# Plain float32 products in place of three products of split operands, in one layer of attention, convolution and mixture of experts

## The chip, the cores and the metric

The kernel runs on one NeuronCore of a Trainium2 chip. The metric is the device time of one execution, in microseconds (us). The names of the engines are those of the profile: PE is the tensor engine's matrix products (PEld its weight loads, which run beside them), DVE the vector engine, ACT the scalar engine, POOL the GpSimd engine, SP the sync engine, which here only issues DMAs.

## The reference

One layer over 1024 tokens of width 1024, all in float32. Cut to what matters here:

```python
h = rmsnorm(x, norm1_g) * (1 + sc1) + sh1              # sh1, sc1, gt1, ...: from c by one product (adaLN)
z = h @ w_in                                           # 1024 x 3744
q_lat, kv_lat, k_rope, conv_in, gate_logits = split(z) # 384, 256, 32, 1024, 2048 columns
q  = rmsnorm(q_lat, q_norm_g) @ w_uq                   # 8 heads of 64 + 32 (the 32 are rotated)
kv = rmsnorm(kv_lat, kv_norm_g) @ w_ukv                # 8 heads of 64 (keys) + 64 (values)
y_attn = causal_attention(q, k, v) @ w_o_attn          # 512 -> 1024
u = glu_a * sigmoid(glu_b)                             # glu_a, glu_b: the halves of conv_in
u = silu(layernorm(causal_depthwise_conv(u, 31 taps)))
y_conv = u @ w_conv_out                                # 512 -> 1024
g_attn, g_conv = split(sigmoid(gate_logits))
x = x + gt1 * ((g_attn * y_attn + g_conv * y_conv) @ w_out)
h = rmsnorm(x, norm2_g) * (1 + sc2) + sh2
# 32 experts in 4 groups: each token takes its best group, and in it its best 2 experts
x = x + gt2 * sum_over_2(weight * (silu(h @ e_gate) * (h @ e_up)) @ e_down)  # 1024 -> 128 -> 1024
out = rmsnorm(x, final_norm_g)
```

## The kernel before

**How float32 products are made.** The tensor engine has two ways to take 32-bit operands: as plain float32, and as the type float32r, a float32 whose low bits don't count. The kernel before makes most of its large products out of float32r operands. Each operand A is kept as two tiles, a high part Ah (ACT casts A to float32r) and a low part Al = A - Ah (a subtraction on POOL or DVE), and the product A B is added up in PSUM from three passes, Ah Bh, Ah Bl and Al Bh. That is `mm3` (L104 to L107); below it is called a triple. The names of the tiles end in h and l: hT0h, hT0l, wg0h, wg0l and so on. A triple makes 128 x 512 outputs out of 128 terms each, except where another width is said. The transposes, the products of the attention's probabilities with the values (mo), the experts' gate and up products (pe) and the router's are plain float32 already.

**The stages, in the order of the program, with their span in the profiled execution and their triples:**

- *0 to 65 us.* x is loaded, normalised and transposed. DVE and PE compute the adaLN vectors as their weights arrive. hT is the normalised, modulated and transposed x in two halves of tokens (n = 0, 1). The first products of the convolution's input start: 32 triples, written as `prod_h` and `prod_l` (L593, L600: lines L597, L598, L603 in the trace).
- *65 to 154 us.* The rest of the convolution's input: for each of 4 blocks of channels j and each half n two products of 8 triples (pa and pb), 96 triples. A GLU (`glu`, L543) makes u[j] from pa and pb, and DVE then goes through the 31 taps of the depthwise convolution (`conv_taps`, L748; one instruction of 128 x 1024 per tap and block, L757), which go on until 292 us. The weights are loaded and split by `wtile` (L507) and `w_split` (L503). The latents' weights wl are split here too (L783 on ACT, L784 on POOL).
- *154 to 214 us.* The latents z (L792): for each of 8 tiles of tokens one product of 384 columns and one of 288, 8 triples each.
- *214 to 416 us.* The 2 x 1024 branch gates (L868 on): 16 blocks of columns by 2 halves by 8 triples, 256 triples. The tanh of each goes to DRAM (gscr). When 6 blocks are issued, the convolution's output cacc is transposed (cT, L834), normalised, and turned into the split tiles csh and csl.
- *416 to 471 us.* `conv_out` (L923): 64 triples, whose result times the gate goes to DRAM (mscr). The latents come back, are normalised and transposed into split tiles; the weights of queries, keys and values are prepared and split.
- *471 to 659 us.* Attention: 16 triples for keys, 48 for queries, 16 for values; the scores (`softmax`, L1046) take 48 triples of 512 columns and 16 each of 384, 256 and 128. Each query, key and attention output is split in turn.
- *659 to 716 us.* The merge (from L1315): the attention's projection w_o_attn, 64 triples (pm), times the gates from DRAM, plus the convolution's branch. The sum yT is split. `split_wout` (L1308) scales each block of w_out by gt1 and splits it.
- *716 to 830 us.* The output projection (`out_mm`, L1486; po): 128 triples. The residual, second norm and router of a tile run beside the products of later tiles.
- *830 to 842 us.* The routing of the last tile and the tables of tokens by expert; `keep_warm` (L1397) issues plain float32 products of no use (warmmm, warmtr) while PE would wait.
- *842 to 1053 us.* The experts (`expert`, L1635), 28 of them one by one with up to 128 rows: gather the rows by an indirect DMA (xg, POOL), transpose them (xp), modulate (xT), gate and up products (pe), the hidden values hid on ACT and DVE, their split (hdh, hdl), the split of the down weights (rdh, rdl: L1654, L1655), two groups of triples of 512 columns for the down product (pd), the scaled result ob on DVE, and an indirect DMA that adds its rows to yscr in DRAM (L1705). The last 4 experts share two blocks of rows; their results are kept on chip as split tiles kh and kl.
- *1053 to 1094 us.* For each tile of tokens the kept rows are added by products with a 0-1 matrix km (pk, L1842: kh and kl, two passes each), then the final norm.

**What sets the order.** Within `manual_schedule` (the loads on SP throughout, the start, the attention's and the output projection's PE work) the program's order is the engine's order. Elsewhere a scheduler orders the instructions of each engine when the program is built, by a simulated timeline. Tiles with one tag share a number of buffers; named slots S0 to S17, R0 to R19 and W0 to W8 of 4 KB per partition are handed on from use to use, and a slot's new tile waits for the last reader of the old one. `seq` (L1431) lists the slots into which the experts' weights are loaded, in order; its first entries are loaded ahead, before the routing is known.

Of the kernel before, what the change touches and what calls it, by code (L numbers as in the profile page):

```python
# [15 lines left out]
F32R = mybir.dt.float32r  # L16
# [35 lines left out]
def hybrid_layer(ctx: ExitStack, tc: tile.TileContext, x, c, positions, ada_w, ada_b, norm1_g,  # L52
# [106 lines left out]
    # constants  # L159
# [24 lines left out]
    # vectors that are wanted as columns: one stack of rows, one transpose  # L184
# [27 lines left out]
    # rotary tables, [token, tile, frequency]  # L212
# [73 lines left out]
    # positions: mask of the diagonal blocks, and whether the tiles follow one another  # L286
# [42 lines left out]
    hpool, hpool_s = open_pool("hpool", "left")  # L329
    hT = [[hpool.tile([P, KD, 512], F32R, name=f"hT{n}{s}") for s in "hl"] for n in range(2)]  # L330
# [28 lines left out]
    def x_square(t):  # L359
        A.activation(hT[1][1][:, 2 * (t % 4):2 * (t % 4) + 2].rearrange("p a b -> p (a b)"), xts[t], AF.Square,  # L360
                     accum_out=ms[:, t:t + 1])
# [16 lines left out]
    def x_trans(n, k):  # L378
        p = ps_tr(f"xT{n}{k}")
        for i in range(4):  # L380
            PE.transpose(p[:, i * P:(i + 1) * P], xts[4 * n + i][:, k * P:(k + 1) * P], ident)
        xn[n, k] = sb.tile([P, 512], F32, name=f"xn{n}{k}", tag="xn", bufs=8)
        return p
# [15 lines left out]
    def ada_load(j):  # L399
# [3 lines left out]
                  3: [(sa, "raw", 3), (sb, "b4", 3)] + [(sa, "raw", 3)] * 2, 4: [(cvp, "cu", 4)] * 4}[j]  # L403
# [96 lines left out]
    def lo_part(lo, full, hi, eng=G):  # L500
        eng.tensor_tensor(lo, full, f32(hi), op=OP.subtract)

    def w_split(w, hi, lo):  # L503
        A.copy(hi, w)
        lo_part(lo, w, hi)

    def wtile(name, src, split=True, parts=1, raw=None):  # L507
        w = (raw or sa).tile([P, KD, P], F32, name=name, tag="b4" if raw else "raw", bufs=3)
# [40 lines left out]
    def conv_w2(j, split=True, parts=1, raw=None):  # L549
        return (w_cols(f"wa{j}", C0 + j * P, split, parts, raw), w_cols(f"wb{j}", C0 + CC + j * P, split, parts, raw))  # L550
# [11 lines left out]
    # loads, in the order in which they are wanted  # L562
# [1375 lines left out]
```

## Time and profile before

| what | value |
|---|---|
| time, median of 3 runs | 1100.92 us |
| lowest, highest | 1093.43, 1104.52 us |
| span of the profiled execution | 1093.9 us |
| PE, DVE, ACT, POOL busy in it | 995.7, 796.1, 437.3, 422.0 us |
| mean granted TensorE clock in it | 0.95 of full speed |

The span is the time from the profiled execution's first instruction to its last; no other time is given for that execution. It is 0.5 us above the lowest of the three runs and 7.0 us below their median. Busy times of different engines overlap. A matmul record lasts longer than the time until the next one starts, since matmuls are pipelined: what a product costs is read from start to start.

### The profile page before, as it was taken

The page shows a single profiled execution, that of the slowest core. Times are in us where ns is not written, and L with a number is a line of the kernel's source. Part 1 is how long each engine was busy: PE and PEld are TensorE (multiplying, and loading weights), DVE is VectorE, ACT ScalarE, POOL GpSimd, SP SyncE. Part 2 cuts the span into 40 slices and gives each one's busy share as a digit, 9 for nine tenths or more (in the row PEclk, how much of TensorE's full clock was granted, in tenths as well). Part 3 has the DMA queues.
Part 4 walks back from the last instruction along what each step waited for, and adds up shares of the span by engine and source line. Part 5 has one row for each costly group of instructions (what it writes and reads, how often), then busy time and mean ns, then how long its engine had stood idle before and what let it go on. Part 6 is the DMA issues. An engine that isn't in the chain of part 4 may idle for free. (4 is left out here: it accounts for less than half of the span.)

```text
span 1093.9 us, 16693 instructions
## 1 busy us (share of the span) xinstructions
PE 995.7 (91%) x5744; PEld 841.5 (77%) x5744; DVE 796.1 (73%) x1839; ACT 437.3 (40%) x914; POOL 422.0 (39%) x361
## 2 busy tenths in 40 slices
PE   4697979999599999999999998899998999999991
PEld 2576869988477788778888877678886999997881
DVE  7989999999989815547556665964447888875555
ACT  4453312212123334347666773232223555543343
POOL 5555929823121114114333446630004464454111
PEclk9798989999899999999999999999999999997876
DMA  9902521246574263710000016684656989998813
GB/s 305 307 8 58 140 70 37 92 159 183 172 228 140 105 213 130 249 41 1 1 2 17 6 59 200 212 300 163 258 189 240 314 284 282 301 272 227 269 77 155
DMA packets 97743, 176.79 MB, mean 162 GB/s; under 512 B 14123, under 2 KB 53116, under 8 KB 97648
## 3 DMA queue, kind: packets, MB, share of 16 engines
q1 hardware_dynamic: 82736, 148.33, 40.8%
q0 software_dynamic: 9152, 16.28, 6.3%
q10 hardware_dynamic: 5760, 11.01, 2.8%
q8 instruction: 48, 0.79, 0.3%
q14 instruction: 47, 0.39, 0.1%
HBM read 145.22 MB, written 40.35 MB: 170 GB/s over the span
## 5 line engine op out<-in xcount | busy, mean ns | idle before, releaser
L757 DVE SCALAR_TENSOR_TENSOR cacc<-u,cw,cacc 128x1024 f32<-128x1024 f32 x120 | 173.2, 1496 | 0.0
L1676 PE MATMUL pe<-xT,rg 128*128 128x128 f32 (+7 forms) x512 | 78.9, 288 | 0.1
L1676 PEld LDWEIGHTS pe<-xT,rg 128*128 128x128 f32 x512 | 73.2, 204 | 5.6 <-ACT xT L1671 0.5
L1671 ACT ACTIVATE xT<-xp,h2c 128x128 f32<-128x128 f32 (+7 forms) x128 | 52.4, 434 | 53.4 <-DVE xT L1668 28.8
L1676 PE MATMUL pe<-xT,ru 128*128 128x128 f32 (+7 forms) x512 | 68.8, 293 | 0.0
L1676 PEld LDWEIGHTS pe<-xT,ru 128*128 128x128 f32 x512 | 66.0, 209 | 0.0
L1705 POOL DMA_INDIRECT yscr<-ob,srci x18 | 33.6, 1868 | 59.4 <-DVE ob L1699 30.4
L105 PE MATMUL po<-woh,y 128*128 128x512 f32 x128 | 53.7, 419 | 1.4 <-DVE gm L1331 1.4
L1668 DVE TENSOR_SCALAR xT<-xp,h2c 128x128 f32<-128x128 f32 (+7 forms) x128 | 45.4, 381 | 10.3 <-ACT xT L1671 9.9
L107 PE MATMUL po<-woh,y 128*128 128x512 f32 x128 | 50.4, 394 | 0.0
L106 PE MATMUL po<-wol,y 128*128 128x512 f32 x128 | 50.3, 393 | 0.0
L873 ACT ACTIVATE gt<-pg 128x512 f32<-128x512 f32 x32 | 19.0, 594 | 68.9 <-PE pg L107 68.9
L1518 POOL TENSOR_SCALAR x1n<-x,rst 128x1024 f32<-128x1024 f32 x8 | 9.0, 1121 | 93.9 <-DVE rst L127 82.4
L479 DVE SCALAR_TENSOR_TENSOR acc<-aw,cact,acc 128x1024 f32<-128x1024 f32 x28 | 39.8, 1421 | 3.2 <-DMA aw<-in_ada_w_dram 3.2
L1663 PE MATMUL xp<-ident,xg 128*128 128x128 f32 (+7 forms) x256 | 39.0, 276 | 1.8 <-DMA xg<-xscr,si 1.8
L1655 DVE TENSOR_TENSOR rdl<-rd,rdh 128x1024 fp32r<-128x1024 f32 x30 | 36.7, 1223 | 5.3 <-ACT rdh L1654 5.2
L1654 ACT CAST rdh<-rd 128x1024 fp32r<-128x1024 f32 x30 | 31.4, 1045 | 18.9 <-PE pd L107 17.8
L1081 PE MATMUL mo<-pT,V 128*64 128x128 f32 x576 | 38.5, 278 | 0.0
L1699 DVE SCALAR_TENSOR_TENSOR ob<-pd,wvp,gt2b 128x512 f32<-128x512 f32 (+7 forms) x36 | 26.4, 744 | 16.6 <-DMA yscr<-ob,srci 12.5
L1663 PEld LDWEIGHTS xp<-ident,xg 128*128 128x128 f32 (+7 forms) x256 | 33.5, 194 | 4.0 <-DVE eid L1619 2.6
L1332 POOL TENSOR_TENSOR gm<-gm 128x512 f32<-128x512 f32 x16 | 27.5, 1726 | 22.0 <-DVE gm L1331 19.4
L1081 PEld LDWEIGHTS mo<-pT,V 128*64 128x64 f32 x576 | 30.8, 136 | 5.7 <-issue 5.7
(2071 smaller groups left out, 3141.2 us busy)
## 6 DMA issues: line engine op xcount, KB each, us to landing
aw<-in_ada_w_dram SPq DMA_DIRECT2D x32, 512.0 KB, 3.8
rg<-in_expert_w_gate_dram SPq DMA_DIRECT2D x32, 512.0 KB, 9.6
ru<-in_expert_w_up_dram SPq DMA_DIRECT2D x32, 512.0 KB, 9.2
rd<-in_expert_w_down_dram SPq DMA_DIRECT2D x32, 512.0 KB, 9.3
x<-in_x_dram SPq DMA_DIRECT2D x16, 512.0 KB, 5.5
ad<-in_ada_w_dram SPq DMA_DIRECT2D x32, 256.0 KB, 5.5
wg<-in_w_in_dram SPq DMA_DIRECT2D x16, 512.0 KB, 4.9
gscr<-gt ACTq DMA_DIRECT2D x32, 256.0 KB, 2.9
```

What stands on the lines that cost most here:

```text
L105: PE.matmul(ps, lh, rh, start=first, stop=False)
L106: PE.matmul(ps, lh, rl, start=False, stop=False)
L107: PE.matmul(ps, ll, rh, start=False, stop=last)
L479: V.scalar_tensor_tensor(acc, w, cact[:, k:k + 1], acc, op0=OP.mult, op1=OP.add)
L757: V.scalar_tensor_tensor(a, u[j][:, k:k + T], cw[:, j, k:k + 1], a, op0=OP.mult, op1=OP.add)
L1081: PE.matmul(po[par * DV:(par + 1) * DV, i % 4 * P:(i % 4 + 1) * P], Vt[b][:, 2 * pr + par], pTs[par][:, b * P:(b + 1) * P], start=(b == 0) ...
L1655: V.tensor_tensor(rdl, rd, f32(rdh), op=OP.subtract)
L1663: PE.transpose(p[:, c], xv[:, k, :], ident[:m, :m])
L1668: split_.append(V.tensor_scalar(xT[:, ks], p[:, c], h2c[:, 0, k:k + 1], h2c[:, 1, k:k + 1], op0=OP.mult, op1=OP.add).ins)
L1671: A.activation(xT[:, ks], p[:, c], AF.Identity, scale=h2c[:, 0, k:k + 1], bias=h2c[:, 1, k:k + 1])
L1676: PE.matmul(pa[:, o:o + m], w[:, k * P:(k + 1) * P], xT[:, k * P:k * P + m], start=(k == 0), stop=(k == KD - 1))
L1705: s_ = G.indirect_dma_start(out=yscr, out_offset=bass.IndirectOffsetOnAxis(ap=src[:m], axis=0), in_=ob[:m], in_offset=None, bounds_check=T ...
```

## The change

Every triple becomes one `PE.matmul` of plain float32 operands. With it go the split tiles, the casts on ACT that made the high parts and the subtractions on POOL and DVE that made the low parts; single float32 tiles take their places. With the room this leaves:

- `raw`, the buffers of the input projection's weights, are 9 instead of 3 (the split tiles wh and wl had 4 each); the latents' weights have places of their own; `conv_out` has 5 buffers for weights and gates instead of 3; the merge has 4 places for its gates instead of 3.
- The slots W0 to W8 are opened before the attention instead of after it, and w_o_attn is loaded into W0 to W3, one load each, where it stayed split in W0 to W7 by way of W8.
- yT takes 8 slots instead of 16, and w_out 8 instead of 16; half of yT's sums move from POOL to DVE. The factor 0.5 that went into yT's split goes into gt1.
- `seq` gives 37 slots before one is used again, instead of 32.
- The kept experts' products pk are one float32 product in place of two float32r passes (kh, kl).

The order of the stages stays. The diff, cut to one place of each kind:

```diff
-    def mm3(ps, lh, ll, rh, rl, first, last):
-        PE.matmul(ps, lh, rh, start=first, stop=False)
-        PE.matmul(ps, lh, rl, start=False, stop=False)
-        PE.matmul(ps, ll, rh, start=False, stop=last)
...
     def second_half(k, p):
-        A.activation(xn[1, k], p, AF.Identity, scale=s1[:, k:k + 1], bias=ada[:, k:k + 1])
-        A.copy(hT[1][0][:, k], xn[1, k])
-        lo_part(hT[1][1][:, k], xn[1, k], hT[1][0][:, k])
+        A.activation(hT[1][:, k], p, AF.Identity, scale=s1[:, k:k + 1], bias=ada[:, k:k + 1])
...
-    def w_split(w, hi, lo):
-        A.copy(hi, w)
-        lo_part(lo, w, hi)
...
     def proj_k(p, w, n, k):
-        mm3(p, w[0][:, k], w[1][:, k], hT[n][0][:, k], hT[n][1][:, k], k == 0, k == KD - 1)
+        PE.matmul(p, w[:, k], hT[n][:, k], start=k == 0, stop=k == KD - 1)
...
     for k in range(KD):
-        w = sa.tile([P, NL], F32, name=f"wl{k}", tag="raw", bufs=3)
+        w = sl.tile([P, NL], F32, name=f"wl{k}")
         SY.dma_start(w, w_in2[k * P:(k + 1) * P, :NL])
-        hi = sl.tile([P, NL], F32R, name=f"wlh{k}")
-        lo = sl.tile([P, NL], F32R, name=f"wll{k}")
-        A.copy(hi, w)
-        G.tensor_tensor(lo, w, f32(hi), op=OP.subtract)
-        wl.append((hi, lo))
+        wl.append(w)
...
     def proj_query(tg, h, n, latT, q, v):
         p = bank(f"{tg}uq{h}{n}", "up", 2)
         for k in range(3):
-            mm3(p, wq[k][0][:, h], wq[k][1][:, h], latT[n][0][:, k], latT[n][1][:, k], k == 0, k == 2)
-        V.tensor_tensor(v, p, tabs[h % 2][:, n * 512:(n + 1) * 512], op=OP.mult)
-        A.copy(q[0], v)
-        G.tensor_tensor(q[1], v, f32(q[0]), op=OP.subtract)
+            PE.matmul(p, wq[k][:, h], latT[n][:, k], start=k == 0, stop=k == 2)
+        V.tensor_tensor(q, p, tabs[h % 2][:, n * 512:(n + 1) * 512], op=OP.mult)
...
             V.scalar_tensor_tensor(g, g, 1.0, p, op0=OP.add, op1=OP.mult)
-            G.tensor_tensor(g, g, gm_[:, 1], op=OP.add)
-            A.activation(hi, g, AF.Copy, scale=0.5)
-            V.scalar_tensor_tensor(lo, g, 0.5, f32(hi), op0=OP.mult, op1=OP.subtract)
+            (V if m % 2 else G).tensor_tensor(yT[m, n], g, gm_[:, 1], op=OP.add)
...
-            A.copy(rdh, rd)
-            V.tensor_tensor(rdl, rd, f32(rdh), op=OP.subtract)
...
         V.scalar_tensor_tensor(hid, hid, 1.0, pa[:, :m], op0=OP.add, op1=OP.mult)
-        V.tensor_tensor(hid, hid, pa[:, P:P + m], op=OP.mult)
-        hid_last[0] = A.copy(hdh, hid).ins
-        V.tensor_tensor(hdl, hid, f32(hdh), op=OP.subtract)
+        V.tensor_tensor(hd, hid, pa[:, P:P + m], op=OP.mult)
...
-                    for e, (kh, kl, km, _) in kept.items():
-                        for w in (kh, kl):
-                            PE.matmul(p, km[:, rows_of(t)], w[:, sl_], start=(e == 0 and w is kh),
-                                      stop=(e == KEEP // 2 - 1 and w is kl))
+                    for e, (kf, km, _) in kept.items():
+                        PE.matmul(p, km[:, rows_of(t)], kf[:, sl_], start=e == 0, stop=e == KEEP // 2 - 1)
```

What stands on PE where the latents end (pz, the latents' product; wl and hT its operands) and the gates begin (pg), before:

```order
L105 MATMUL pz_1862<-wlh_1362,hT1h 128x288
L106 MATMUL pz_1862<-wll_1363,hT1h 128x288
L107 MATMUL pz_1862<-wlh_1362,hT1l 128x288
L105 MATMUL pz_1862<-wlh_1368,hT1h 128x288
L106 MATMUL pz_1862<-wll_1369,hT1h 128x288
L107 MATMUL pz_1862<-wlh_1368,hT1l 128x288
L105 MATMUL pg_1928<-hT0h,wg0h 128x512
L106 MATMUL pg_1928<-hT0l,wg0h 128x512
L107 MATMUL pg_1928<-hT0h,wg0l 128x512
```

And there after the change (x8: eight instructions of this kind in a row):

```order
L722 MATMUL pz_1252<-wl_996,hT_139 128x288
L722 MATMUL pz_1252<-wl_998,hT_139 128x288
L722 MATMUL pz_1252<-wl_1000,hT_139 128x288
L505 MATMUL pg_1300<-hT_138,wg_1298 128x512 x8
L505 MATMUL pg_1312<-hT_139,wg_1298 128x512 x8
L505 MATMUL pg_1326<-hT_138,wg_1324 128x512 x8
```

Three instructions became one at each step; the order of the products is the same.

What stands on POOL ahead of the rotation of the shared key (rt), in the stretch in which DVE goes through the taps, before (wll and wg: the subtractions of the latents' and the gates' weights; three more of wll and those of the convolution's weights stand ahead of these):

```order
L784 TENSOR_TENSOR wll_1345<-wl_1342,wlh_1344 128x672
L784 TENSOR_TENSOR wll_1351<-wl_1348,wlh_1350 128x672
L784 TENSOR_TENSOR wll_1357<-wl_1354,wlh_1356 128x672
L784 TENSOR_TENSOR wll_1363<-wl_1360,wlh_1362 128x672
L784 TENSOR_TENSOR wll_1369<-wl_1366,wlh_1368 128x672
L501 TENSOR_TENSOR wg0l<-wg_1922,wg0h 128x1024
L501 TENSOR_TENSOR wg1l<-wg_1984,wg1h 128x1024
L501 TENSOR_TENSOR wg2l<-wg_2046,wg2h 128x1024
L501 TENSOR_TENSOR wg3l<-wg_2108,wg3h 128x1024
L772 TENSOR_TENSOR rt_1429<-z_1372,cosT 128x16
```

And there after the change (the rows from the last of POOL's share of the norm of x on):

```order
L363 TENSOR_SCALAR x_166<-x_166,rstd 128x1024
L520 MEMSET u_559 128x30
L520 MEMSET u_561 128x30
L520 MEMSET u_563 128x30
L520 MEMSET u_565 128x30
L706 TENSOR_TENSOR rt_1027<-z_1002,cosT 128x16
```

All subtractions are gone from POOL; until the first latent is there it has only small things to do.

What stands on PE in the middle of the experts, from one expert's gate and up products (rg, ru) through another's down product (pd) to the next gate product, before:

```order
L1676 MATMUL pe_11285<-xT_11204,rg_9987 128x128 x3
L1676 MATMUL pe_11285<-xT_11204,ru_9989 128x128 x8
L105 MATMUL pd_11308<-rdh_11111,hdr 128x512
L106 MATMUL pd_11308<-rdl_11112,hdr 128x512
L105 MATMUL pd_11313<-rdh_11111,hdr 128x512
L106 MATMUL pd_11313<-rdl_11112,hdr 128x512
L107 MATMUL pd_11308<-rdh_11111,hdr 128x512
L107 MATMUL pd_11313<-rdh_11111,hdr 128x512
L1676 MATMUL pe_11347<-xT_11266,rg_9993 128x128 x3
```

And after the change (hid: the hidden values):

```order
L1525 MATMUL pe_8452<-xT_8381,rg_7345 128x128 x4
L1525 MATMUL pe_8452<-xT_8381,ru_7347 128x128 x8
L1545 MATMUL pd_8473<-rd_7343,hid_8022 128x512
L1545 MATMUL pd_8476<-rd_7343,hid_8022 128x512
L1525 MATMUL pe_8504<-xT_8433,rg_7351 128x128 x2
```

Two instructions stand where six stood, and they read the loaded weights rd and hid themselves.

## Rows read from the trace of the kernel before

**Rows 1.** The page's head and part 1: busy time of each engine.
```profile
span 1093.9 us, 16693 instructions
PE 995.7 (91%) x5744; PEld 841.5 (77%) x5744; DVE 796.1 (73%) x1839; ACT 437.3 (40%) x914; POOL 422.0 (39%) x361
```

**Rows 2.** Stages: length; busy PE, PEld, DVE, ACT, POOL; granted clock, DMA share, GB/s.
```profile
0.00:65.30 65.30, 40.01 (x155) 30.44 (x156) 56.83 (x148) 27.88 (x56) 32.98 (x54) 0.90 0.84 259
65.30:154.20 88.90, 76.66 (x332) 61.78 (x331) 83.96 (x113) 30.74 (x43) 54.17 (x23) 0.92 0.28 73
154.20:213.70 59.50, 58.91 (x386) 58.65 (x385) 59.50 (x54) 16.59 (x47) 47.03 (x43) 1.00 0.14 48
213.70:415.60 201.90, 185.56 (x838) 151.55 (x837) 164.31 (x227) 49.67 (x81) 43.99 (x21) 0.97 0.55 171
415.60:470.60 55.00, 52.49 (x257) 42.04 (x256) 30.99 (x54) 22.17 (x40) 13.81 (x8) 1.00 0.60 199
470.60:659.40 188.80, 183.06 (x1396) 152.55 (x1394) 113.11 (x488) 124.73 (x284) 72.81 (x83) 1.00 0.04 14
659.40:715.90 56.50, 50.18 (x208) 39.84 (x209) 44.80 (x46) 17.53 (x30) 37.76 (x49) 0.94 0.67 218
715.90:829.80 113.90, 113.16 (x607) 94.46 (x608) 56.86 (x274) 29.89 (x75) 14.58 (x12) 1.00 0.64 238
...
842.40:1053.10 210.70, 208.45 (x1474) 192.44 (x1475) 148.28 (x336) 99.77 (x226) 91.90 (x61) 0.91 0.87 268
1053.10:1093.90 40.80, 17.12 (x71) 12.79 (x69) 26.69 (x57) 15.74 (x30) 7.21 (x3) 0.79 0.26 104
```

**Rows 3.** Timeline of PE amid the gates: start, us, instruction.
```profile
249.76 0.39 PE L105 MATMUL pg<-hT0h,wg3h 128*128 128x512 f32 x1
...
250.44 0.39 PE L105 MATMUL pg<-hT0h,wg3h 128*128 128x512 f32 x1
```

**Rows 4.** Timeline of PEld in the warm-up products: each float32 product loads twice.
```profile
837.44 0.19 PEld L1402 LDWEIGHTS warmtr<-gt2b,ident 128*128 128x128 f32 x1 [0.24 <-issue]
839.58 0.19 PEld L1402 LDWEIGHTS warmtr<-gt2b,ident 128*128 128x128 f32 x1 [0.24 <-issue]
```

**Rows 5.** Chain that ended last: start, us, and what ran (an expert's products).
```profile
881.73 2.46 PE pe L1676 x22
887.56 2.46 PE pe L1676 x22
```

**Rows 6.** Waits of PE: us in total, times, longest.
```profile
PE pb L105 <- DVE u L546: 12.2, 2, 6.5
PE cT L834 <- DVE cacc L757: 11.6, 1, 11.6
PE pm L105 <- DVE gm L1331: 5.0, 3, 2.3
```

**Rows 7.** Timelines of DVE's taps and of POOL beside them.
```profile
108.48 16.77 DVE L757 SCALAR_TENSOR_TENSOR cacc<-u,cw,cacc 128x1024 f32<-128x1024 f32 x7
188.17 8.45 DVE L757 SCALAR_TENSOR_TENSOR cacc<-u,cw,cacc 128x1024 f32<-128x1024 f32 x7
...
108.91 20.44 POOL L784 TENSOR_TENSOR wll<-wl,wlh 128x672 fp32r<-128x672 f32 x8 [2.29 <-ACT wlh L783]
```

**Rows 8.** Group of the page's part 5: all taps; busy us, mean ns, idle before.
```profile
L757 DVE SCALAR_TENSOR_TENSOR cacc<-u,cw,cacc 128x1024 f32<-128x1024 f32 x120 | 173.2, 1496 | 0.0
```

**Rows 9.** Timeline of PE: one expert's down product.
```profile
901.44 0.48 PE L105 MATMUL pd<-rdh,hdr 128*128 128x512 f32 x1
...
902.91 0.27 PE L1676 MATMUL pe<-xT,rg 128*128 128x128 f32 x1
```

**Rows 10.** The end in two stretches, columns as in rows 2.
```profile
1053.00:1072.60 19.60, 16.69 (x70) 12.73 (x70) 16.81 (x31) 10.68 (x22) 6.30 (x3) 1.00 0.13 54
1072.60:1082.70 10.10, 0.53 (x3) 0.09 (x1) 9.88 (x27) 5.15 (x9) 0.91 (x1) 0.71 0.63 250
```

More of the change, by code (lines that the diff above doesn't have):

```diff
@@ L329, in hybrid_layer @@
     hpool, hpool_s = open_pool("hpool", "left")
-    hT = [[hpool.tile([P, KD, 512], F32R, name=f"hT{n}{s}") for s in "hl"] for n in range(2)]
+    hT = [hpool.tile([P, KD, 512], F32, name=f"hT{n}") for n in range(2)]
     cvp, cvp_s = open_pool("cvp", "right")
@@ L698, in hybrid_layer @@
     pt = {}
-    prod_h((0, 1), 0, ka)
-    prod_l((0,), 0, ka)
-    prod_h((0,), 0, kb)
-    prod_l((0,), 0, kb)
-    for i in range(4):
-        if i in TR:
-            pt[len(pt)] = x_trans(1, len(pt))
-        if i < 3:
-            (prod_l, prod_h, prod_l)[i]((1,), 0, (ka, kb, kb)[i])
+    prod((0, 1), 0, ka)
+    prod((0,), 0, kb)
+    for i in range(2):
+        pt[len(pt)] = x_trans(1, len(pt))
+    prod((1,), 0, kb)
     u_tiles()
@@ L791, in hybrid_layer @@
             for k in range(KD):
-                hh, hl = (hT[n][s][:, k, i * P:(i + 1) * P] for s in range(2))
-                mm3(p[:, :c1 - c0], hh, hl, wl[k][0][:, c0:c1], wl[k][1][:, c0:c1], k == 0, k == KD - 1)
+                PE.matmul(p[:, :c1 - c0], hT[n][:, k, i * P:(i + 1) * P], wl[k][:, c0:c1], start=k == 0, stop=k == KD - 1)
             A.copy(z[:, c0:c1], p[:, :c1 - c0])
@@ L827, in hybrid_layer @@
     cs = []
+    lgh = pro.tile([P, 8], F32, name="lgh")
+    V.tensor_scalar_mul(lgh, cols[:, R_LG:R_LG + 8], 0.5)
     def conv_stats():
@@ L903, in hybrid_layer @@
     lp, lp_s = open_pool("lp", "left")
-    latT = [[lp.tile([P, 5, 512], F32R, name=f"lat{n}{s}") for s in "hl"] for n in range(2)]
+    latT = [lp.tile([P, 5, 512], F32, name=f"lat{n}") for n in range(2)]
     def load_lat(tg, alloc, bank_, latT, halves):
@@ L935, in conv_out @@
             for k in range(4):
[L936 removed]
+                PE.matmul(p, w[:, k], cs[k][:, sl_], start=k == 0, stop=k == 3)
             V.scalar_tensor_tensor(g, g, 1.0, p, op0=OP.add, op1=OP.mult)
@@ L1129, in hybrid_layer @@
         for k in range(2):
-            lh, ll = (latT[n][s][:, 3 + k, i * P:(i + 1) * P] for s in range(2))
-            mm3(p, lh, ll, wv[0][:, k].rearrange("p h e -> p (h e)"), wv[1][:, k].rearrange("p h e -> p (h e)"),
-                k == 0, k == 1)
+            PE.matmul(p, latT[n][:, 3 + k, i * P:(i + 1) * P], wv[:, k].rearrange("p h e -> p (h e)"),
+                      start=k == 0, stop=k == 1)
         A.copy(Vt[t].rearrange("p h e -> p (h e)"), p)
@@ L1221, in fbig @@
             return fb.tile([P, T], dt, name="f" + name, tag=tag, bufs=bufs)
-        flat_ = [[fb.tile([P, 5, 512], F32R, name=f"flat{n}{s}") for s in "hl"] for n in range(2)]
+        flat_ = [fb.tile([P, 5, 512], F32, name=f"flat{n}") for n in range(2)]
         load_lat("f", lambda nm: fb.tile([P, QL + KL], F32, name=nm, tag=("s", "pt", "pt", "mk")[int(nm[3:]) % 4],
@@ L1257, in hybrid_layer @@
                 take(pr, n, po)
-        for cc in range(4):
-            split_att(cc, 0)
         fb_s.close()
@@ L1270, in hybrid_layer @@
         slot_of[f"R{i}"] = (rp, f"R{i}")
-    for cc in range(4):
-        at = slot(f"at{cc}1", f"R{4 + cc}", [P, 2, 512], F32R)
-        aT[cc, 1] = (at[:, 0], at[:, 1])
-        split_att(cc, 1)
     def bc_row(name, sl_, r):
@@ L1487, in out_mm @@
         n_, i_ = divmod(t, 4)
-        yh, yl = (yT[k, n_][s][:, i_ * P:(i_ + 1) * P] for s in range(2))
         sl_ = slice(n * 512, (n + 1) * 512)
-        mm3(ps, yh, yl, wov[k][0][:, sl_], wov[k][1][:, sl_], k == 0, k == KD - 1)
+        PE.matmul(ps, yT[k, n_][:, i_ * P:(i_ + 1) * P], wov[k][:, sl_], start=k == 0, stop=k == KD - 1)
     x1s, x1T, x1n, pss, lgs, x1_in, h_out = {}, {}, {}, {}, {}, [], []
@@ L1696, in expert @@
             p = bank(f"pd{nm}{n}", "pd", 4)[:rows]
-            for a, (h_, l_, wh, wl) in enumerate(parts):
-                mm3(p, h_, l_, wh[:, sl_], wl[:, sl_], a == 0, a == len(parts) - 1)
+            for a, (h_, w_) in enumerate(parts):
+                PE.matmul(p, h_, w_[:, sl_], start=a == 0, stop=a == len(parts) - 1)
             V.scalar_tensor_tensor(ob[:rows, sl_], p, wcol[:rows], gt2b[:rows, sl_], op0=OP.mult, op1=OP.mult)
-            if keep:
-                A.copy(keep[0][:, sl_], ob[:, sl_])
-                V.tensor_tensor(keep[1][:, sl_], ob[:, sl_], f32(keep[0][:, sl_]), op=OP.subtract)
         if keep:
```

285 lines of the change are left out of this document (87 added, 198 removed).

## Prediction

> **What bounds the kernel now.** I read the page's head first [rows 1]: PE is busy for 995.7 of 1093.9 us, so there are 98.2 us in which it has nothing to do, and no other engine comes near it over the whole. Then the stages [rows 2]. In five of them PE leaves under 6 us: the latents 0.6 (59.5 less 58.91), `conv_out` 2.5, the attention 5.7, the output projection 0.7, the experts 2.3. There every added microsecond of PE is added to the time. PE has slack in four: 25.3 us in the start, 12.2 in the convolution's input, 16.3 in the gates, 6.3 in the merge; and at the end, 23.7. The waits of PE say who is late there [rows 6]: DVE with the GLU's u (12.2 us), DVE with the last taps (11.6 us), DVE with the merge's gm (5.0 us). The clock column of rows 2 is the third thing to see: 0.92, 0.97 and 0.94 in the stages with these waits, 1.00 where PE has none. A mean of 0.92 between the two levels of 1.2 and 2.4 GHz means that some 16% of the stage ran at the lower one.
>
> **What a product costs, before and after.** A triple goes from 249.76 to 250.44 us: 0.68 us, 0.227 a pass [rows 3]. A plain float32 product of 128 x 512 stands in the same trace, in the warm-up, and takes two matmul records: five records from 837.44 to 839.58, 0.428 each, 0.856 us for the product [rows 4]. So the edit that saves two instructions of three makes the product dearer by 0.176 us. The experts show the same rate for narrow products: 22 records of up to 128 columns in 2.46 us, 0.112 each, and 5.84 us from expert to expert [rows 5]. Between 128 and 512 columns I take a straight line: a record of 384 is 0.323, one of 288 is 0.244 us.
>
> This case's float32 product is thus 3.8 passes long. The Trainium skill, "FP8 and Floating Point Precision", section "TensorE Precision Notes", gives four passes for true float32. By that page and a price of 0.227 a pass a product would be an estimated 0.908 us, and the sum below 43 us more; the row of 0.856 is a measurement, so I use it, and keep the other as a rival.
>
> **The change, stage by stage**, in span (triples from the code, 512 columns unless said).
>
> *Start, to 65.3 us:* 32 triples, +5.6 us of PE, but PE idles for 25.3 and DVE is busy for 56.83 of 65.30 at a DMA share of 0.84 [rows 2]. The splits on ACT and POOL ahead of the first products go. Cover: the loads and DVE's adaLN sums; if it weren't there, +5.6. I take +1.
>
> *Convolution's input, 88.9 us:* 96 triples, +16.9. PE is busy for 76.66, and its two waits of 12.2 are for DVE, whose queue is slowed by POOL: beside POOL's subtractions a tap takes 2.40 us (16.77 / 7), later 1.21 (8.45 / 7) [rows 7]. With the subtractions gone from POOL, DVE is early, the waits go and with them the lower clock: of its 14 us (16% of 88.9) I count 9 as work of PE, done at half the rate, so -4.5. 76.66 + 16.9 - 4.5 = 89: I take 0, and bounds of -4 and +17.
>
> *Latents:* 64 pairs of 384 and 288 columns now take 59.5 / 64 = 0.930; after 2 x (0.323 + 0.244) = 1.134, 72.6 in all: +13. Nothing hides it.
>
> *Gates:* 256 triples, +45.1. The wait of 11.6 for the taps goes: 120 taps are busy for 173.2 us [rows 8], where 120 at 1.21 would be 145, so DVE can be done up to 28 us earlier, and PE arrives 14 us later. Then what is late next is PE itself, whose remaining slack is under 5 us. With 2 us for the clock that the wait had cost: +31.
>
> *`conv_out`:* 64 triples, +11.3, of which the 2.5 us of slack takes a part: +9.
>
> *Attention:* 128 triples, +22.5; 48 narrower ones +3. Against it: a group of float32r passes amid float32 work pays for the change of form. The six passes of a down product take 1.47 us, 0.11 over six times 0.227 [rows 9]; at 0.08 for each of some 88 groups here (my choice, the groups being shorter) that is -7. +18.5. The ACT, DVE and POOL work that goes lay beside PE.
>
> *Merge:* 64 triples, +11.3, less 6.3 of slack and 3 of lower clock (0.94 of 56.5 us): +2. What would be late next is the gates' loads (DMA share 0.67).
>
> *Output projection:* 128 triples, +22.5; PE is full (113.16 of 113.9), the groups are cut up by transposes, -3.5 for the changes of form: +19.
>
> *Routing:* no triple, 0.
>
> *Experts:* a down product goes from 1.47 to 2 x 0.856 = 1.71, +0.24; 28 of them +7, 8 triples of the kept ones +1. A scatter needs its ob, so the chain through DVE shortens by the splits but DMA (0.87) stays. The mean clock of 0.91 means some 38 us at the lower level: if that went, -19; if it doubled, +19. I take -3: +5.
>
> *End:* 64 passes become 32 products: by the pass of 0.23 14.7 us, after 27.4, +12.7. But DVE sets the end: behind PE's last product it still works for 10.1 us without a gap (9.88) [rows 10]. After the change a tile of tokens costs PE 3.4 us and DVE 3.3 (26.69 / 8), so DVE keeps up, and one tile of about 4 us is left after the last product; the split of the kept rows ahead of pk saves 1.5. +12.7 - 6 - 1.5: +5.
>
> Sum: 1 + 0 + 13 + 31 + 9 + 18.5 + 2 + 19 + 0 + 5 + 5 = 103.5; span 1197. The profiled execution stands with the lowest of the three runs, the median is 7 us above; I add 3 and say 1200.
>
> **Bounds.** All PE work added, with nothing hidden: 832 triples x 0.176 = 146, the latents 13, narrow scores 3, the end 13, less 14 for changes of form (32 down groups included) = 161, span 1255. All 98.2 us of PE's idle time used up: 63, span 1157.
>
> **Rivals.**
>
> *More is taken back.* The lower clock goes as well, everywhere: what the stages of rows 2 lack to 1.00, times their lengths, is some 50 us in all. 161 - 98 - 50 = 13: span 1107. For it: the waits and the clock stand together in rows 2. Against it: the start waits for loads, and the end has no products to fill it. Between 1115 and 1155: 0.05.
>
> *Each float32 record costs what a float32r pass does.* A product would then be 0.46, and 832 of them save 183 us. The start and the convolution's input, 128 triples, couldn't use it as DVE is full there, and the taps would hold the gates up more: some 45 us less, so about 960. It decides as soon as a product costs under 0.68. For it: the records of rows 4 are of one kind of operand, a constant one. Against it: the experts' narrow records give the same rate. 0.03.
>
> *Four passes of 0.227.* 1243, as worked out above. The records of the warm-up speak against it. 0.03.
>
> *The clock drops more often.* In the experts, where the lower level comes back at 0.91: 19 us more, 1219 for that stage alone, and with a second stage of the kind above 1240. Against it: PE gets more to do, not less. Above 1240: 0.04.
>
> *The change hides itself:* all that PE gains in work, it loses in waits of the three queues. That would need 161 us to go where 148 are to be had, counting the clock: within 1%, 0.03.
>
> **How the numbers follow.** The forecast, 1155 to 1240, has the rest, 0.82. The range is that. Nothing under 1155 but above no change alters the sign, so slower by over 1% (about what a measurement of this kernel can tell from none) gets 0.94, the same 0.03, faster 0.03.
>
> **What would show it.** Right: product starts in the gates at 0.86 us; the latents at 72 us; no wait of PE for u or cacc; taps at 1.2 throughout; pd groups of 1.71; DVE done soon after the last pk. Wrong: product starts of 0.46 or 0.91; a wait for cT that stays; a granted clock under 0.9 in a stage that now has 1.00; an output projection that grows by less than 15 or more than 25 us.

## The result and the profile after

The changed kernel takes 1200.26 us (median of 4 runs, 1199.37 to 1202.82) against 1099.04 for the kernel before beside it: ratio 1.0928, 95% interval 1.0885 to 1.0971. The forecast was 1200, in a range of 1155 to 1240. The profiled execution spans 1197.6 us; the forecast's span was 1197. The total is met much more closely than its terms, which is why the terms are gone through below.

The page's head and part 1 of the changed kernel, as [rows 1] of the one before:

```profile
span 1197.6 us, 14032 instructions
PE 1137.3 (95%) x4736; PEld 657.7 (55%) x4736; DVE 631.4 (53%) x1705; ACT 315.7 (26%) x720; POOL 251.4 (21%) x273
```

PE has 142 us more to do, with 1008 instructions fewer; DVE has 165 us less, ACT 122, POOL 171. PE's idle time fell from 98.2 to 60.3 us, and 142 less 38 is the 104 by which the span grew.

The stages of the changed kernel (columns as in [rows 2]); each begins with the first product of its kind, the last but two with the first warm-up product, the last with the first of the unbroken run of pk:

```profile
0.00:150.40 150.40, 130.99 (x358) 62.98 (x359) 110.26 (x272) 32.99 (x59) 10.20 (x39) 0.95 0.56 163
150.40:232.60 82.20, 74.98 (x258) 49.74 (x257) 76.79 (x74) 14.74 (x44) 65.42 (x37) 0.96 0.11 37
232.60:461.30 228.70, 227.74 (x580) 103.80 (x579) 108.31 (x187) 31.87 (x57) 3.48 (x13) 1.00 0.45 148
461.30:523.70 62.40, 62.16 (x193) 30.95 (x192) 20.53 (x46) 14.48 (x30) 0.00 (x0) 1.00 0.51 173
523.70:733.60 209.90, 205.06 (x1219) 124.96 (x1217) 91.23 (x458) 116.36 (x265) 47.84 (x65) 1.00 0.03 11
733.60:792.10 58.50, 58.50 (x145) 26.78 (x146) 26.60 (x32) 2.19 (x7) 24.82 (x44) 0.97 0.75 267
792.10:928.10 136.00, 135.26 (x491) 72.56 (x490) 51.70 (x272) 25.62 (x69) 9.73 (x9) 1.00 0.48 180
928.10:938.60 10.50, 7.41 (x24) 3.23 (x23) 8.15 (x40) 0.69 (x3) 5.28 (x6) 1.00 0.42 148
938.60:1152.20 213.60, 207.28 (x1418) 170.61 (x1419) 112.83 (x272) 62.47 (x162) 77.10 (x60) 0.97 0.84 264
1152.20:1197.60 45.40, 27.90 (x63) 12.04 (x61) 24.97 (x54) 14.35 (x27) 7.52 (x3) 0.84 0.24 94
```

The last four stages of the kernel before, cut at the same events (the cuts differ a little from those of [rows 2]):

```profile
715.90:831.00 115.10, 114.36 (x618) 95.66 (x618) 57.88 (x279) 29.89 (x75) 14.58 (x12) 1.00 0.64 240
831.00:842.40 11.40, 8.92 (x23) 3.77 (x22) 9.73 (x42) 2.57 (x5) 5.77 (x6) 0.85 0.45 160
842.40:1056.40 214.00, 210.48 (x1483) 193.79 (x1483) 149.74 (x339) 100.62 (x228) 91.90 (x61) 0.91 0.85 263
1056.40:1093.90 37.50, 15.09 (x62) 11.44 (x62) 25.22 (x55) 14.89 (x28) 7.21 (x3) 0.77 0.29 113
```

With the other stages from [rows 2], in us:

| stage | before | after | change | forecast |
|---|---|---|---|---|
| start and convolution's input | 154.2 | 150.4 | -3.8 | +1 |
| latents | 59.5 | 82.2 | +22.7 | +13 |
| gates | 201.9 | 228.7 | +26.8 | +31 |
| `conv_out` | 55.0 | 62.4 | +7.4 | +9 |
| attention | 188.8 | 209.9 | +21.1 | +18.5 |
| merge | 56.5 | 58.5 | +2.0 | +2 |
| output projection | 115.1 | 136.0 | +20.9 | +19 |
| routing | 11.4 | 10.5 | -0.9 | 0 |
| experts | 214.0 | 213.6 | -0.4 | +5 |
| end | 37.5 | 45.4 | +7.9 | +5 |
| sum | 1093.9 | 1197.6 | +103.7 | +103.5 |

The price of a product shows in the weight loads amid the gates (start, us, instruction), as [rows 4] did for the warm-up:

```profile
300.36 0.19 PEld L505 LDWEIGHTS pg<-hT,wg 128*128 128x128 f32 x1 [0.24 <-issue]
...
302.51 0.19 PEld L505 LDWEIGHTS pg<-hT,wg 128*128 128x128 f32 x1 [0.24 <-issue]
```

Five records in 2.15 us, 0.43 each and 0.86 a product. Of PE's waits that [rows 6] had, those for u, cacc and gm are gone. Two are new behind the start:

```profile
PE pz L722 <- ACT z L723: 7.2, 1, 7.2
PE pe L1525 <- DMA ru<-in_expert_w_up_dram: 5.5, 1, 5.5
```

And one is much shorter, that for DVE's sums of the adaLN (ac), before and after; a new one for DVE's hT (5.6 us in four waits) takes back a part:

```profile
PE pf L442 <- DVE ac L433: 12.0, 4, 6.9
...
PE pf L435 <- DVE ac L426: 2.4, 2, 1.4
```

The first of the two new waits is the surprise of this profile. Timelines of four engines in the latents show where it comes from:

```profile
159.22 33.56 DVE L691 SCALAR_TENSOR_TENSOR cacc<-u,cw,cacc 128x1024 f32<-128x1024 f32 x28
...
160.14 32.71 POOL L706 TENSOR_TENSOR rt<-z,cosT 128x16 f32<-128x16 f32 x1 [110.34 <-ACT z L723]
192.82 0.21 POOL L707 TENSOR_TENSOR rt<-z,sinT 128x16 f32<-128x16 f32 x1
...
193.43 0.48 ACT L723 COPY z<-pz 128x384 f32<-128x384 f32 x1 [23.79 <-POOL rt L707]
...
193.96 38.75 PE L722 MATMUL pz<-wl,hT 128*128 128x384 f32 x128 [7.22 <-ACT z L723]
```

One product of POOL on 16 columns, which alone takes 0.21 us, lasts 32.71: about as long as DVE goes through 28 taps without a break. It reads z, of which there are two tiles; ACT waits 23.79 us for one of them, PSUM isn't emptied, and PE waits 7.22 us.

The second, for ru, is a matter of SP's order. The eight loads of yscr for the final norm stand ahead of the last expert's up weights, where the kernel before issued them behind all weights (1032.28 us, the last weights at 1029.08):

```profile
1129.00 3.90 SPq L1677 DMA_DIRECT2D r<-yscr  x8
1133.49 0.34 SPq L1304 DMA_DIRECT2D ru<-in_expert_w_up_dram  x1
```

### The profile page after: what moved, and what is told of

The parts are those of the page before. It is cut to its first block, busy times and chain, and to the rows that moved or that the text cites. A ratio compares the mean times of both kernels' runs of the same rounds, so it can differ in the third digit from the quotient of the medians.

```text
span 1197.6 us, 14032 instructions
## 1 busy us (share of the span) xinstructions
PE 1137.3 (95%) x4736; PEld 657.7 (55%) x4736; DVE 631.4 (53%) x1705; ACT 315.7 (26%) x720; POOL 251.4 (21%) x273
## 5 line engine op out<-in xcount | busy, mean ns | idle before, releaser
L505 PE MATMUL pg<-hT,wg 128*128 128x512 f32 x512 | 221.8, 592 | 0.0
L505 PEld LDWEIGHTS pg<-hT,wg 128*128 128x128 f32 x512 | 96.3, 190 | 116.7 <-issue 116.3
L1349 PE MATMUL po<-wo,y 128*128 128x512 f32 x256 | 117.7, 600 | 0.0
L722 PE MATMUL pz<-wl,hT 128*128 128x384 f32 (+1 forms) x256 | 75.1, 457 | 7.2 <-ACT z L723 7.2
L1349 PEld LDWEIGHTS po<-wo,y 128*128 128x128 f32 x256 | 45.6, 190 | 42.6 <-issue 42.6
L706 POOL TENSOR_TENSOR rt<-z,cosT 128x16 f32<-128x16 f32 x16 | 43.9, 2744 | 117.5 <-ACT z L723 117.3
L722 PEld LDWEIGHTS pz<-wl,hT 128*128 128x128 f32 x256 | 49.7, 195 | 32.8 <-ACT z L723 7.7
L1196 PE MATMUL pm<-att,wp 128*128 128x512 f32 x128 | 57.1, 608 | 3.7 <-ACT shm L1167 3.7
L856 PE MATMUL pc<-cs,wc 128*128 128x512 f32 x128 | 56.1, 592 | 0.0
L1545 PE MATMUL pd<-rd,hid 128*128 128x512 f32 (+7 forms) x112 | 52.8, 594 | 0.0
```

Of the source, the lines that this page charges most:

```text
L505: PE.matmul(p, w[:, k], hT[n][:, k], start=k == 0, stop=k == KD - 1)
L706: eng.tensor_tensor(a[:, s], src[:, s * NF:(s + 1) * NF], cosb, op=OP.mult)
L722: PE.matmul(p[:, :c1 - c0], hT[n][:, k, i * P:(i + 1) * P], wl[k][:, c0:c1], start=k == 0, stop=k == KD - 1)
L856: PE.matmul(p, w[:, k], cs[k][:, sl_], start=k == 0, stop=k == 3)
L1196: PE.matmul(p, wov_[k][:, m * P:(m + 1) * P], attT[k][:, sl_], start=k == 0, stop=k == 3)
L1349: PE.matmul(ps, yT[k, n_][:, i_ * P:(i_ + 1) * P], wov[k][:, sl_], start=k == 0, stop=k == KD - 1)
```

## The experiments

Two theories stand against each other for the main effect: that the price of a product makes the time (the forecast's), and that the moved slots, loads and order do. Then there are the single stages that came out otherwise than forecast.

**The price by itself (p1_price).** The kernel before, with every triple made one product, all side work kept (`prod_h` and `prod_l` likewise; the low parts don't enter the products):

```diff
-        PE.matmul(ps, lh, rh, start=first, stop=False)
-        PE.matmul(ps, lh, rl, start=False, stop=False)
-        PE.matmul(ps, ll, rh, start=False, stop=last)
+        PE.matmul(ps, f32(lh), f32(rh), start=first, stop=last)
```

> The kernel before, with each triple replaced by one float32 product that reads the high tiles as plain float32; all casts and subtractions are still done, and the low parts are left out of the products. Theory (the price of a float32 product, 0.856 against 0.68 us, makes the change's time, and the side work lay beside PE): 1190 to 1215 us, near the changed kernel's 1200, with output projection, conv_out and latents as long as there (136, 62, 73 us without a new wait). Rival A (a good part of the 100 us comes from the changed slots, loads and order): under 1170. Rival B (taking the side work away had hidden a still larger price): over 1225.

Measured: 1232.07 us, 1.1184 [1.1114, 1.1254], in the range of rival B. Four stages of this kernel (latents, gates, output projection, experts) say why:

```profile
164.30:255.20 90.90, 78.06 (x258) 51.16 (x257) 88.27 (x81) 16.35 (x47) 72.67 (x42) 0.91 0.11 37
255.20:502.80 247.60, 231.88 (x581) 106.52 (x580) 129.46 (x197) 50.31 (x81) 46.46 (x24) 0.97 0.46 139
837.80:973.90 136.10, 135.36 (x492) 72.65 (x490) 57.12 (x280) 29.77 (x75) 16.25 (x13) 1.00 0.55 201
985.00:1188.90 203.90, 203.18 (x1414) 167.40 (x1412) 151.35 (x338) 103.68 (x227) 83.56 (x60) 1.00 0.91 276
```

The output projection takes 136.1 us, the changed kernel 136.0: there the price is all. Latents and gates take 28 us more than in the changed kernel, and its start, to 164.3, 14 more; the experts take 10 less. The stages that take longer are those with the taps. Their group in this kernel, and in the next one, where the subtractions of the weights are on DVE:

```profile
L754 DVE SCALAR_TENSOR_TENSOR cacc<-u,cw,cacc 128x1024 f32<-128x1024 f32 x120 | 174.9, 1509 | 0.0
```

```profile
L754 DVE SCALAR_TENSOR_TENSOR cacc<-u,cw,cacc 128x1024 f32<-128x1024 f32 x120 | 147.4, 1273 | 0.0
```

**The price, and the subtractions of the weights on DVE (p3_price_v).** To the edit above this is added:

```diff
-            w_split(w, hi, lo)
+            w_split(w, hi, lo, V)
...
-        G.tensor_tensor(lo, w, f32(hi), op=OP.subtract)
+        V.tensor_tensor(lo, w, f32(hi), op=OP.subtract)
         wl.append((hi, lo))
```

> The kernel of p1_price (one float32 product over the high tiles, the low parts left out of the products but still made) with the subtractions of the later convolution weights, the latents' weights and the gates' weights on DVE instead of POOL. Theory (what p1_price lost against the changed kernel, 32 us, it lost because POOL's subtractions slow DVE's taps, and so PE waited in the input, the latents and the gates): 1195 to 1205 us, the wait for cT under 3 us. Rival (the lost time comes from other splits, the casts on ACT or the fewer buffers): over 1220.

Measured: 1197.82 us, 1.0873 [1.0791, 1.0955]. So what p1_price lost is lost to POOL's subtractions beside the taps, and the change's total comes out inside the kernel before from two of its parts: the price, and a POOL without these subtractions. The other side work that the change removed, and the new slots, are worth about nothing in sum, but by stage they are not: against the changed kernel the start and input are 7.4 us longer here (157.8), the stages from `conv_out` to the merge 6.6 longer together, and all from the first warm-up product on is 16.2 shorter (253.3 in place of 269.5).

**One pass less (p2_two).** The kernel before without the pass that takes the low part of the second operand.

```diff
-        PE.matmul(ps, lh, rl, start=False, stop=False)
```

> The kernel before with one of the three passes left out everywhere (the one with the low part of the second operand of each triple), two passes of 0.227 instead of three. Theory (PE sets the pace from the latents on, DVE before that): the 834 passes gone are worth 189 us on PE, of which the start, the convolution's input and the gates up to the last tap give nothing: 960 to 1010 us. Rival (PE is busy but not the bound; loads and DVE pace it): over 1050.

Measured: 1040.42 us, 0.9444 [0.9401, 0.9487]; outside what either theory expected. Its gates and its experts:

```profile
198.00:391.00 193.00, 134.81 (x579) 107.78 (x577) 179.73 (x234) 49.11 (x80) 43.38 (x32) 0.82 0.53 158
...
754.00:1000.00 246.00, 221.10 (x1438) 199.63 (x1436) 155.66 (x376) 100.72 (x231) 98.73 (x66) 0.81 0.77 236
```

In the gates PE idles for 58 of 193 us behind a DVE that is 93% busy, and the granted clock is 0.82; in the experts it idles for 25 and has 0.81. The experts got longer by it: with their warm-up they take 247.0 us, where the kernel before has 225.4 for 64 passes more. The output projection went down by 17.5 us, from 115.1 to 97.6, where the 128 passes less are worth 29. So PE is the bound for added work in nearly every stage, and soon not the bound for work taken away.

**The latents (a1_rope_v, a2_z4).** In the changed kernel, the rotation of the shared key on DVE, and in another run two more buffers for z (its tag is shared, so the GLU's tanh tiles and one of the adaLN sums get four as well):

```diff
-        rope(G, kpe[:, t], z[:, QL + KL:], cosT[:, t], sinT[:, t],
+        rope(V, kpe[:, t], z[:, QL + KL:], cosT[:, t], sinT[:, t],
```

> The changed kernel with the rotation of the shared key (48 small products on 16 columns) on DVE instead of POOL. Theory (POOL's small products can't start while DVE goes from tap to tap; the z tiles are held by them, ACT can't empty PSUM, and PE waits 7.2 us and then has the lower clock for a while): the latents go from 82 to 73 us, the time falls by 8 to 10 us to 1190 to 1193. Rival (a float32 product of 384 and 288 columns is itself dearer than the straight line): latents 82 us as now, time 1200.

Measured: 1194.43 us, 1.0841 [1.0796, 1.0885], just outside what was expected of the time.

```diff
-        z = sa.tile([P, NL], F32, name=f"z{t}", tag="th", bufs=2)
+        z = sa.tile([P, NL], F32, name=f"z{t}", tag="th", bufs=4)
```

> The changed kernel with four buffers for z instead of two, POOL's rotation left as it is. Theory (as for the run with the rotation on DVE): POOL's first small product still lasts tens of us beside the taps, but ACT has two tiles more to write; the PE wait of 7.2 us goes, the latents take 73 to 76 us, time 1190 to 1194. Rival: no change, 1200.

Measured: 1191.87 us, 1.0819 [1.0760, 1.0878]. The latents and gates of the first, then of the second:

```profile
150.10:222.40 72.30, 72.30 (x257) 48.63 (x256) 72.30 (x105) 15.71 (x46) 0.00 (x0) 1.00 0.13 41
222.40:456.30 233.90, 229.34 (x580) 104.71 (x579) 116.12 (x205) 31.21 (x54) 0.36 (x1) 0.99 0.46 145
```

```profile
149.20:221.50 72.30, 72.30 (x257) 48.62 (x256) 72.30 (x68) 15.51 (x46) 62.60 (x28) 1.00 0.12 41
221.50:453.00 231.50, 229.02 (x581) 104.84 (x580) 112.50 (x193) 31.32 (x54) 15.50 (x22) 0.99 0.46 147
```

Both bring the latents to 72.3 us with PE full, which is the 72.6 that the straight line of the forecast gave. With four buffers POOL's first product still lasts as long:

```profile
158.90 31.98 POOL L706 TENSOR_TENSOR rt<-z,cosT 128x16 f32<-128x16 f32 x1 [109.76 <-ACT z L723]
```

So it is the two tiles of z that carry POOL's delay to PE. Of the 9.9 us won, 5.2 and 2.8 come back in the gates, where PE idles for 4.6 and 2.5 us in place of 1.0. Its longest waits there are for ACT's copies of the transposes (cT for tokn: 4.6 and 2.5 us, 1.0 in the changed kernel), to which it comes at 304.81 and 303.90 us in place of 314.95. That these waits are longer because PE comes earlier fits, but no run shows it by itself. The intervals of the two times end about where the changed kernel's begins (1.0885); the stages show the effect more clearly.

**The end (a3_pk_split).** The changed kernel with the kept rows split into kh and kl again, two float32r passes each:

```diff
-                        PE.matmul(p, km[:, rows_of(t)], kf[:, sl_], start=e == 0, stop=e == KEEP // 2 - 1)
+                        for w in (kh, kl):
+                            PE.matmul(p, km[:, rows_of(t)], w[:, sl_], start=(e == 0 and w is kh),
+                                      stop=(e == KEEP // 2 - 1 and w is kl))
```

> The changed kernel with the kept experts' rows split again into kh and kl and added in two float32r passes each (64 passes of 0.23 us in place of 32 products of 0.856). Theory (after the change PE, not DVE, paces the end): the stretch from the first of the last products to the end goes from 45.3 back to 37 to 39 us, the time falls by 6 to 8 us to 1192 to 1194. Rival (DVE and the output's DMA set the end in both): 45 us, 1200.

Measured: 1192.33 us, 1.0823 [1.0783, 1.0863]. The end takes 38.2 us in place of 45.4: after the change PE paced it.

```profile
1151.70:1189.90 38.20, 16.07 (x63) 11.64 (x62) 25.96 (x56) 14.95 (x28) 7.20 (x3) 0.77 0.28 111
```

**The last expert's weights (a4_loads).** The changed kernel with the loads of yscr behind them:

```diff
+    with tc.issue_after(last_load[0]):
         for t in range(NT):
             SY.dma_start(r0[t], yscr[rows_of(t), :])
```

> The changed kernel with the eight loads of yscr put behind the last expert's weights in SP's queue. Theory (they were put ahead of the last up and down weights, whose load then came late and cost PE a wait of 5.5 us and some lower clock behind it): no wait of PE for ru, 5 to 8 us less, 1192 to 1195. Rival (the weights' slot came free late anyway, or the rows then come late for the norm): 1198 to 1202.

Measured: 1192.22 us, 1.0822 [1.0783, 1.0862]. No wait of PE for ru is left, and from the first warm-up product to the run of pk it takes 215.3 us (930.4 to 1145.7) in place of 224.1.

**The subtractions, in the kernel before (b1_sub_v).** With only the second edit of p3_price_v, all triples kept:

> The kernel before with the subtractions of the later convolution weights, the latents' weights and the gates' weights on DVE instead of POOL. Theory (a subtraction on POOL doubles the time of the taps beside it, so that POOL's 3 us cost DVE more than the 1.1 us it would take itself): taps of 1.2 us throughout, the waits of 12.2 and 11.6 us shrink, 1080 to 1092 us. Rival (DVE gets as much to do as it wins): 1095 to 1105.

Measured: 1068.36 us, 0.9670 [0.9617, 0.9723]: more than the theory expected. The taps and the latents' subtractions as groups of the trace:

```profile
L757 DVE SCALAR_TENSOR_TENSOR cacc<-u,cw,cacc 128x1024 f32<-128x1024 f32 x120 | 148.0, 1287 | 0.0
...
L784 DVE TENSOR_TENSOR wll<-wl,wlh 128x672 fp32r<-128x672 f32 x8 | 6.9, 862 | 0.0
```

And the first three stages:

```profile
0.00:138.30 138.30, 111.93 (x487) 89.10 (x487) 124.26 (x272) 58.67 (x99) 45.45 (x62) 0.95 0.56 166
138.30:203.20 64.90, 61.15 (x385) 60.92 (x384) 60.44 (x57) 15.28 (x44) 49.61 (x35) 0.95 0.16 53
203.20:385.50 182.30, 182.30 (x837) 150.70 (x836) 157.25 (x236) 48.47 (x78) 4.83 (x15) 1.00 0.58 178
```

The latents' eight subtractions, which POOL made in 20.44 us [rows 7], take DVE 6.9; with those of the convolution's and the gates' weights moved as well (28 in all), the taps lose 25 us of busy time against [rows 8]. The stages to the gates' end come to 385.5 us, 30.1 less than before; both waits, for u and for cacc, are gone. The latents grew by 5.4: POOL's rotation is held up here too (22.29 us for one product).

**Only the latents' subtractions (b6_wl_v):**

> The kernel before with only the eight subtractions of the latents' weights on DVE. Theory (the gain of 34 us of b1_sub_v goes by the time for which POOL reads beside the taps): these are 20 of some 40 us of subtractions beside the taps, so 12 to 20 us less, 1083 to 1090. Rival (the gain comes from the convolution's weights, on which PE waits directly): 1096 to 1102.

Measured: 1086.98 us, 0.9867 [0.9792, 0.9942], as the theory expected and outside the rival's range. So the gain goes, roughly, by the time for which POOL reads beside the taps; the taps are busy for 161.7 us here, between 173.2 and 148.0, and about half of each wait of PE is left (6.5 for u, 5.6 for cacc).

**The experts alone as float32, in the kernel before (b2_exp):**

```diff
-            for a, (h_, l_, wh, wl) in enumerate(parts):
-                mm3(p, h_, l_, wh[:, sl_], wl[:, sl_], a == 0, a == len(parts) - 1)
+            for a, (h_, w_) in enumerate(parts):
+                PE.matmul(p, h_, w_[:, sl_], start=a == 0, stop=a == len(parts) - 1)
```

> The kernel before with the experts' down products alone as plain float32 products of the unsplit weights and hidden values; the kept rows stay split. Theory (a down product costs PE 0.24 us more, but with the splits gone no wait of some 2 us lets the clock fall to its lower level for the last 55 us of the experts): 8 to 12 us less, 1087 to 1093, granted clock 1.00 in the experts in place of 0.91. Rival (price alone): 7 us more, 1105 to 1108, clock as before.

Measured: 1097.70 us, 0.9970 [0.9945, 0.9995]: a smaller gain than expected. The clock rose to 0.97, but a new wait of 5.0 us for the last up weights took most of it, the same as in the changed kernel. Here too the loads of yscr are issued ahead of these weights (1033.44 and 1037.62 us), although `seq` is the old one.

**Together (b5_rope).** In the kernel before: the subtractions and the rotation on DVE, the experts' down products float32, the loads of yscr behind the weights.

> The kernel before with b1_sub_v's subtractions on DVE, b2_exp's float32 down products in the experts, the rotation of the shared key on DVE, and the loads of yscr behind the last expert's weights; the triples stay everywhere else. Theory (these are separate waits, and each goes): b1_sub_v's 1068 less 4 to 5 for the latents' wait and 5 to 10 for the experts: 1053 to 1062. Rival (the waits hide one another): 1063 to 1069.

Measured: 1056.28 us, 0.9586 [0.9541, 0.9632], faster than both kernels. Its profiled execution spans 1051.9 us. The stages to the gates' end, and from the warm-up to pk:

```profile
0.00:138.20 138.20, 112.87 (x487) 90.52 (x488) 124.67 (x272) 59.05 (x99) 45.91 (x62) 0.91 0.56 166
138.20:196.80 58.60, 58.60 (x385) 58.60 (x384) 58.60 (x92) 16.66 (x47) 0.00 (x0) 1.00 0.18 58
196.80:380.90 184.10, 182.38 (x838) 150.70 (x836) 161.79 (x246) 45.79 (x72) 0.00 (x0) 1.00 0.55 167
...
799.80:1015.10 215.30, 211.39 (x1442) 170.87 (x1441) 123.13 (x315) 64.76 (x168) 82.62 (x66) 0.99 0.86 262
```

The latents are full at 58.6 us, and warm-up and experts take 215.3 where the kernel before has 225.4.

And in the changed kernel (a6_all): four buffers for z, the kept rows split, the loads of yscr behind the weights.

> The changed kernel with four buffers for z, the kept rows split for the last products, and the loads of yscr behind the last expert's weights. Theory (the three gains of 8 us each are in different stages and add up): 1174 to 1180 us. Rival (they overlap): 1184 to 1190.

Measured: 1182.49 us as the median of four runs, two at 1172.78 and 1175.57 and two at 1189.40 and 1191.89; without the slowest of them the ratio is 1.0721 [1.0622, 1.0821]. By the time this is undecided between the two, and what parts the pairs is not shown; in the profiled execution (span 1173.4, one of the faster pair) each of the three gains is there: latents 72.3, warm-up and experts 215.2, end 37.2 us.

## Why the prediction was right, and where its terms were not

*The price.* Right: 0.856 us for a product out of the warm-up's records, 0.86 in the changed kernel, and the same in the output projection of two kernels (136.0, 136.1 us). The two rivals that hung on another price (0.46, 0.908) fall with it. Those by which waits or the clock would give back much more, or all, fall by PE's idle time, which went down by 38 of its 98 us; the one by which the clock drops more often falls by the mean clock, which rose from 0.95 to 0.98. The estimate by the four passes of the Trainium skill, "FP8 and Floating Point Precision", section "TensorE Precision Notes", at 0.227 each would have put the time at 1243; the trace has 0.86, less than four of this kernel's passes.

*Stages where PE is full after the change.* The output projection (+20.9 for +19), the attention (+21.1 for +18.5), `conv_out` (+7.4 for +9) and the merge (+2.0 for +2) are right but for one size: the gain for the changes of form was taken as 3.5 and 7 us. The attention's PE work grew by 22.0 (183.06 to 205.06), 3.5 under the 25.5 of the price; the output projection's by 20.9, 1.6 under 22.5. So these gains were half as large, if they are what the shortfall is; no run takes the changes of form by themselves.

*The latents: +22.7 for +13.* The term's price was right (72.3 us when nothing disturbs), but the sign that was named, latents at 72 us, didn't come. "Nothing hides it" was true, but the step left out a wait. It said that with the subtractions gone DVE is early; it didn't ask what DVE's unbroken taps do to the POOL work that stays. The new wait is 7.2 us, and the lower clock (0.96, PE busy for 74.98 us in place of 72.30) makes up the rest of the 9.9.

*Start and input: -3.8 for +1.* The input's mechanism was right, and p3_price_v, b1_sub_v and b6_wl_v show it: POOL's subtractions slow the taps, and PE waits for u behind them. Its size was about right as well: 15.9 us when the triples stay (154.2 to 138.3), where the sum took back 12.2 and 4.5. The miss is in the start, which the sum took to be covered by DVE's adaLN sums. These sums are slowed by POOL too: five subtractions of 1.7 us each run beside the six steps of the first line, none beside those of the second, from the changed kernel:

```profile
28.89 8.13 DVE L429 SCALAR_TENSOR_TENSOR ac<-ad,cact,ac 128x512 f32<-128x512 f32 x6
...
27.72 4.06 DVE L422 SCALAR_TENSOR_TENSOR ac<-ad,cact,ac 128x512 f32<-128x512 f32 x6
```

As these sums got faster, PE's wait for ac went from 12.0 to 2.4 us. Where the subtractions of the first weights stayed on POOL it stayed too (10.5 in p3_price_v, 11.9 in b1_sub_v), and the start and input of p3_price_v are 157.8 us; no run moves these subtractions alone.

*Gates: +26.8 for +31.* With the latents' wait away it is 231.5 to 233.9, about the forecast's 232.9. So this miss goes with that of the latents. The sum had left PE an idle time of under 5 us here; in the changed kernel 1.0 is left of 16.3. (The taps of the kernel before go on until 310 us, not 292 as its description has it; its wait of 11.6 us ends when those are done that the first transposes read.)

*Experts: -0.4 for +5.* The +8 of price was hidden by the clock: PE's busy time fell by 3.2 (210.48 to 207.28), while the mean clock rose from 0.91 to 0.97. The sum took 3 us for that and named 19 as the bound. The prediction read the lower clock as going with the waits, but this stage had 0.91 with 2.3 us of idle time [rows 2]. The 5.5 us for ru took back a part; without it the stage with its warm-up is 8.8 shorter. The new order of SP's loads was not asked for. It isn't the new `seq` that makes it, since b2_exp has it with the old one: it comes with the experts' splits gone.

*End: +7.9 for +5.* Right in kind: PE now paces it, and with the split kept the end is 38.2. The price was right too (PE busy 12.8 us longer, for 12.7); 4.9 us of it were hidden, where the sum took 7.5.

The errors of the terms, +9.7 in the latents and -4.8, -4.2 and -5.4 in the start, the gates and the experts, come to -4.7, and the others bring back 4.9. A total within 1 us of 104 is luck by that much.

## What to carry to other kernels

Read the price of a replacement from a row of the same trace where there is one, even a warm-up, and price work added to a stage by PE's slack there; work taken away is another matter, since the next engine is often close (a third of the passes gone gave 6% here). Where DVE runs long rows of instructions with two operands in SBUF, as the taps here, try to keep elementwise work off POOL, or give the tiles that POOL holds more buffers: moving 1 us subtractions to an already busy DVE gained 3% in this kernel. When side work goes, look at what it had slowed and then at what it had held back, and at the loads whose order was set with it.

## What the runs showed of the hardware that was not expected

- A product of POOL on 16 columns waited for a whole unbroken run of DVE's taps: 32.71 us behind 28 taps in the changed kernel, 31.98 with four buffers for z, 22.29 in b1_sub_v behind 18. It isn't POOL's subtractions that decide it: p1_price has them all on POOL, and one product lasts 29.48 us there (at 194.96). The Trainium skill, "SBUF — State Buffer", section "Who interferes with whom", says that a DVE instruction with two inputs in SBUF contends with a GpSimd instruction that reads SBUF, and that the contention is an exclusive lock. The trace agrees in kind, and goes further: POOL didn't get in between two taps either. In the kernel before, by the same trace view, such a product took at most 1.24 us, one tap's length, in an unbroken run of 19 taps as well:

```profile
173.81 22.81 DVE L757 SCALAR_TENSOR_TENSOR cacc<-u,cw,cacc 128x1024 f32<-128x1024 f32 x19
...
178.72 1.24 POOL L773 TENSOR_TENSOR rt<-z,sinT 128x16 f32<-128x16 f32 x1
179.91 1.23 POOL L772 TENSOR_TENSOR rt<-z,cosT 128x16 f32<-128x16 f32 x1
```

  Why it got in there and not here isn't settled by any run.
- With a pass less the granted clock is 0.82 and 0.81 in the gates and experts, with PE idle for 58 and 25 us; the kernel before has 0.97 and 0.91, with 16.3 and 3.5. Idle time in sum isn't all that counts: the experts of the kernel before have the lower clock of these two with the smaller idle time.
